# Mean squares of q and k from two float32r products of squares split in two, in a transformer-like two-layer mixer kernel

## The chip, the cores and the metric

The kernel runs on one core of a Trainium2 chip. The metric is the device time of one execution in microseconds. Several engines work at once, each through its own list of instructions: TensorE (PE) multiplies matrices, VectorE (DVE), ScalarE (ACT) and GpSimd (POOL) work elementwise, and SyncE (SP) issues most transfers. Semaphores hold an instruction back until the data that it needs are there.

## The reference

Two layers treat 1024 latent tokens and 256 prompt tokens of width 1024. A layer computes, for latent and prompt tokens alike:

```
h = rms_norm(x, norm_g) * (1 + scale) + shift        # scale, shift, gate from adaLN
aq, ak, av, ag, bq, bk, bv, bg, cx, cg, ga, gb, gc = split(h @ w_in)
qa, ka = rope(rms_norm(aq, a_qn)), rope(rms_norm(ak, a_kn))   # the prompt is not rotated
ya = attention(qa, ka, av, sink) * silu(ag)          # branch A: window of 128, 8 heads, 2 kv heads
qb, kb = rms_norm(bq, b_qn), rms_norm(bk, b_kn)
yb = attention(qb, kb, bv, bias) * silu(bg)          # branch B: 2-D neighbourhood, 8 heads
yc = lru_scan(conv(cx)) * silu(cg)                   # branch C
z = sigmoid(ga)*(ya @ w_br[0]) + sigmoid(gb)*(yb @ w_br[1]) + sigmoid(gc)*(yc @ w_br[2])
x = x + gate * (z @ w_out)
```

The change concerns the `rms_norm` of q and k: each head has 64 channels, and its vector is divided by the root of the mean of its squares plus 1e-6.

## The kernel before

Activations lie feature-major: 128 channels on the partitions, tokens along the free axis, in three chunks of 512, 512 and 256 tokens (the last is the prompt). Dense products are float32 in effect: weights and activations are each split into two float32r parts, hi and lo, and a product is three float32r products. For the weights ScalarE copies the hi part (line 415) and GpSimd subtracts for the lo part (line 416).

TensorE's order is written by a planner, the class `Weave`. It keeps a clock `now` that each emitted matrix product advances by its planned duration, holds two queues of dense jobs and a heap of steps that become due, and interleaves these with the attention of groups of heads. `W.later(T["ms"], f)` makes f due T["ms"] planned nanoseconds later. The other engines' order is made from the order in which the program emits.

q and k of a pair of heads are computed chunk by chunk in jobs; after the last product of a chunk its `evac` calls `qk_norm` (line 713). ScalarE squares the chunk (line 716), VectorE multiplies it by its gain (717). The step `finish` is due T["ms"] later: TensorE multiplies the squares by `blk`, a float32 constant that averages the 64 channels of each head (line 721). Then VectorE adds eps (723), ScalarE takes Ln and Exp (729, 730), one Newton step follows on both (731 to 734), and in branch A latent chunks are rotated: VectorE shuffles (738) and GpSimd multiplies and adds (739 to 741), with cosines and sines in a tile of tag `stage`. Last, `to_dram` splits the result in two float32r parts on GpSimd (a copy, line 751, and a subtraction, 752) in a tile `st` of tag `stage`, which goes to DRAM. `stage` has two buffers, `qraw` and `qsq` as well.

A layer has 5 jobs for k (four in branch B, one in branch A) and 8 for q. Tiles of chunk c of k and q are named `k_..._c` and `q_..._c`.

Of the kernel before, what the change touches and what calls it, by code (L numbers as in the profile page):

```python
# [9 lines left out]
F32 = mybir.dt.float32  # L10
F32R = mybir.dt.float32r
# [4 lines left out]
P = 128  # L16
# [11 lines left out]
EPS = 1e-6  # L28
# [49 lines left out]
LDB = ("d", "t")  # L78
T = dict(f1=9, f2=2, kc=3000, c0=10000, cq=1, gx=3, nx=3500, yo=1500, yi=1000, aa=2, ab=3, ap=1300, ac=3500, ms=1800, v=3000, tok=8260, scale=1000, t0=3100, tb=2000, o=2000, soft=7000, pace=9000, lg=300, lr=8000, cv=9500, le=4000)


class Weave:
    """Order of the tensor engine's work. A step is emitted once its operands should be there (times are in ns of
    the tensor engine's work); products that wait for nothing fill the time in between."""

# [34 lines left out]

    # the first job of a queue that will need weights
    def loads(self, q):
# [11 lines left out]

    # the weights of the job after this one are fetched while this one runs
    def fetch(self):
# [53 lines left out]
def trunk(nc, tc, ctx, I, K, O):  # L190
    PSUM = bass.MemoryType.PSUM
    DRAM = bass.MemoryType.DRAM
# [5 lines left out]
    cp = ctx.enter_context(pool("const"))  # L198
# [8 lines left out]

    # the loads of the start go out in the order of the program
    def ordered(ins):
# [3 lines left out]
    def f32(ap):  # L213
        return ap.bitcast(F32)

    def mm(out, a, b, start, stop):
        nc.tensor.matmul(out, a, b, start=start, stop=stop)  # L217
        n = 1
        for d in b.shape[1:]:
            n *= d  # L220
        W.now += max(n, 256) / 2.4 * (4 if a.dtype == F32 else 1) + 3
# [7 lines left out]

    # the table that serves both Exp and Ln, from the moment that x is there  # L230
    def exp_ln(x):
# [3 lines left out]

    cst = cp.tile([P, 386], F32, name="cst")
    nc.scalar.dma_start(cst[:, :384], K["k_const"][:, :384])
    nc.scalar.dma_start(cst[:, 384:], K["k_const"][:, 768:])
    ident, blk, ones_d, sel = cst[:, 0:128], cst[:, 128:256], cst[:, 256:384], cst[:, 384:386]
    fill = cp.tile([P, 2], F32, name="fill")  # L240
# [18 lines left out]

# [1 line left out]
    colT, dcol, sink, crows = [], [], [], []  # L261
# [27 lines left out]
    def constants(l):  # L289
        sk, ct, dc = sink[l], colT[l], dcol[l]  # L290
        tc.keep_in_program_order(nc.vector.tensor_scalar(sk[:, 1], sk[:, 0], -1.0, None, ALU.mult))
        # gains (those of q with the score scale) times -1 / 2, gate biases negated or halved
        for i, c in enumerate((-HD ** -0.5, 1.0, -HD ** -0.5, 1.0)):
            nc.vector.tensor_scalar(dc[:, i:i + 1], ct[:, R_QN + i:R_QN + i + 1], -0.5 * c, None, ALU.mult)
        nc.vector.tensor_scalar(dc[:, 4:12], ct[:, R_BA:R_BA + 8], -1.0, None, ALU.mult)
        nc.vector.tensor_scalar(dc[:, 12:20], ct[:, R_BX:R_BX + 8], 0.5, None, ALU.mult)
        # softplus(-lam) = max(-lam, 0) + log1p(exp(-|lam|)), log1p(y) = 2 atanh(y / (2 + y))
        lam = ct[:, R_LAM:R_LAM + 8]
        tmp = cp.tile([P, 40], F32, name=f"sp{l}", tag="sp")
        y, z, z2, acc, mx = (tmp[:, 8 * i:8 * i + 8] for i in range(5))  # L300
        nc.vector.tensor_scalar(mx, lam, -1.0, None, ALU.mult)
        nc.vector.tensor_tensor(y, lam, mx, ALU.min)
        nc.scalar.activation(y, y, AF.Exp)
        nc.vector.tensor_scalar(z, y, 2.0, None, ALU.add)
        nc.vector.reciprocal(z, z)
        nc.vector.tensor_tensor(z, z, y, ALU.mult)
        nc.vector.tensor_tensor(z2, z, z, ALU.mult)
        nc.vector.tensor_scalar(acc, z2, 1.0 / 17, 1.0 / 15, ALU.mult, ALU.add)
        for n in (13, 11, 9, 7, 5, 3, 1):
            nc.vector.tensor_tensor(acc, acc, z2, ALU.mult)  # L310
            nc.vector.tensor_scalar(acc, acc, 1.0 / n, None, ALU.add)
        nc.vector.tensor_tensor(acc, acc, z, ALU.mult)
        nc.vector.tensor_scalar(mx, mx, 0.0, None, ALU.max)
        nc.vector.scalar_tensor_tensor(acc, acc, 2.0, mx, ALU.mult, ALU.add)
        nc.vector.tensor_scalar(dc[:, 20:28], acc, -8.0, None, ALU.mult)
        nc.vector.tensor_scalar(dc[:, 28:36], acc, 8.0, None, ALU.mult)

# [1 line left out]
    mod = [cp.tile([P, 24, 2], F32, name=f"mod{l}") for l in range(DEPTH)]  # L319
# [81 lines left out]

# [1 line left out]
    def load_w(w, c0, name):  # L403
# [27 lines left out]

    # a job: one block of 128 columns of a weight matrix for the tokens of all the chunks
    # (tall: tile by tile of the contraction for all the chunks at once)
    def job(w, c0, chunks, rhs, evac, name, before=None, tall=False):
# [29 lines left out]

    # the modulated input of a layer in two parts, latent and prompt tokens in tiles of their own
    class Hidden:
# [7 lines left out]

        # room that a part of the prompt takes later
        def before(self, i, k, name):
# [19 lines left out]

    # several blocks side by side, so that each tile of H serves them all as soon as it is there
    def wide(w, blocks, ci, H, sp):
# [22 lines left out]

    # rs = (ms + EPS) ** -0.5: by Exp and Ln, then one step of Newton's
    def rstd(rs, ms, tmp):
# [6 lines left out]

# [1 line left out]
    def add_square(l, ci, k, x, acc, add):  # L532
# [29 lines left out]

# [1 line left out]
    def lru(l, H, rp):  # L564
# [4 lines left out]
        tiles = {}  # L569
# [50 lines left out]
        for f in range(4):  # L620
# [17 lines left out]
            A, S = [], []  # L638
            # r = sigmoid; a = exp(log a), log a = -8 softplus(-lam) r
            for d in range(2):  # L640
# [11 lines left out]
            for d in range(2):  # L652
                nc.scalar.activation(R[d], R[d], AF.Tanh, scale=dc[:, 28 + 4 * d + f:29 + 4 * d + f])
                # 1 - a^2 = (1 + a^2) tanh(-log a)
                nc.vector.scalar_tensor_tensor(S[d], S[d], 1.0, R[d], ALU.add, ALU.mult)
# [9 lines left out]
            for d in range(2):  # L665
                # sqrt(1 - a^2) / 2 times (1 + tanh) x = sqrt(1 - a^2) sigmoid x
                nc.scalar.activation(S[d], S[d], AF.Ln, bias=tiny_c, scale=0.25)
# [17 lines left out]

# [1 line left out]
    def gate_evac(dst, name):  # L687
# [18 lines left out]

# [1 line left out]
    def attention(l, H, ap):  # L708
        w_in = I["w_in"][l]
        loaded = []  # L710

        # normalised q and k (rotated in branch A) go to DRAM in two float32r parts
        def qk_norm(ps, N, gain, rope_c0, name, then):
# [3 lines left out]
            nc.vector.tensor_scalar(raw[:, :N], ps, gain, None, ALU.mult)  # L717

            def finish():
                ms = ps_tile("t", f"{name}_ms")  # L720
                mm(ms[:, :N], blk, sq[:, :N], True, True)
                me = cp.tile([P, 512], F32, tag="g2", name=f"{name}_me", bufs=3)
# [4 lines left out]
                rs = sq  # L727
                # one step of Newton's on rs; raw carries its factor -1 / 2
                nc.scalar.activation(rs[:, :N], me[:, :N], AF.Ln)
# [116 lines left out]
        class Keys:  # L846
            """Keys, values and biases of a pair of heads; in branch A all the pairs share keys and values."""

# [46 lines left out]
        class Group:  # L895
            """Heads a, b of a pair, query blocks t0 and t0 + 1; two parts of two units (head, block) each."""

# [24 lines left out]

            # q, masks and biases are negated, so the least score is the negated maximum
            def score(g, s, i):
# [215 lines left out]

# [1 line left out]
    def merge_jobs(l, mp, zpool, rest, swap):  # L1142
        Y, Z, acc, gated, gate = {}, [], [], {}, {}

        # y silu(g), with silu(g) = g (1 + tanh(g / 2)) / 2
        def gate_y(b, f):
# [72 lines left out]
    def output_jobs(l, cis, Z, xp, H, free):  # L1219
# [4 lines left out]
        def evac(k):  # L1224
            def run(ci, ps):
                c0, N = CHUNKS[ci]
                name = f"xo{l}_{ci}_{k}"
                # x of the prompt and its mean square lie where H is written when they are no longer needed
                if last or ci < 2:
# [26 lines left out]

    # half of the features of a chunk goes out, token-major
    def write_out(ci, xs, h):
# [12 lines left out]

# [1 line left out]
    def input_load(ci, sp):  # L1273
# [29 lines left out]

# [1 line left out]
    def bias_tables():  # L1305
# [177 lines left out]
```

## Time and profile before

| | us |
|---|---|
| median of three runs (lowest, highest) | 3311.87 (3310.23, 3314.44) |
| span of the profiled execution | 3318.7 |
| TensorE busy in it | 3198.1 |
| VectorE busy | 1767.1 |
| ScalarE busy | 1675.4 |
| GpSimd busy | 971.7 |

The profile has one execution; what it gives besides is its span, from the first to the last instruction, 0.2% longer than the median of the timed runs. A row of a timeline has a start, a duration, the engine, the line of the kernel and the tiles. Matrix products are pipelined, so that a product's duration in such a row is longer than the time for which it holds TensorE: that is read from one start to the next.

### The profile page before, as it was taken

To read this page: it belongs to the slowest core of one execution; us is meant where nothing else is said; L and a number is where in the kernel's file an instruction comes from. 1 tells how busy PE (TensorE), PEld (TensorE's weight loads), DVE (VectorE), ACT (ScalarE), POOL (GpSimd) and SP (SyncE) were. 2 spreads that over 40 slices of the span, in tenths; PEclk is the share of its full clock that TensorE was granted. 3 is DMA by queue.
4 is the path that set the end of the run, shared out by engine and by line. 5 is a ranking of instruction groups with operands and counts; after the bars stand their busy time and mean duration, and the time that the engine had idled before them with its cause. 6 is when DMAs were issued, how large, how long until landed. Compare 5 with 4: busy or idle time off the path is not lost.

```text
span 3318.7 us, 47971 instructions
## 1 busy us (share of the span) xinstructions
PE 3198.1 (96%) x17419; PEld 2657.4 (80%) x17419; DVE 1767.1 (53%) x3255; ACT 1675.4 (50%) x3565; POOL 971.7 (29%) x827
## 2 busy tenths in 40 slices
PE   8888999999999999999999999999999999999999
PEld 5655678888888888888878777888888888888887
DVE  5545236566665665445453544566656665645531
ACT  5544435555555555544245573455555555544422
POOL 3433332222232220126433233122223221112643
PEclk9989999999999999999999999999999999999999
DMA  8445463454443322365442225454445332337543
GB/s 289 118 103 117 123 185 98 140 158 119 139 144 108 99 83 85 135 215 175 129 135 91 66 69 142 128 146 138 118 143 171 99 92 82 91 103 241 184 145 102
DMA packets 414121, 435.02 MB, mean 131 GB/s; under 512 B 43872, under 2 KB 329148, under 8 KB 412604
## 3 DMA queue, kind: packets, MB, share of 16 engines
q1 hardware_dynamic: 407900, 414.91, 42.1%
q0 software_dynamic: 5664, 16.83, 1.9%
q8 instruction: 137, 2.24, 0.3%
q14 instruction: 100, 0.82, 0.1%
q10 hardware_dynamic: 320, 0.21, 0.0%
HBM read 298.12 MB, written 137.29 MB: 131 GB/s over the span
## 4 chain that ended last, share of the span: by engine, by line
PE 72%; DVE 10%; DMA 6%; ACT 4%; issue 4%; POOL 3%; SPq 1%; ACTq 0%; POOLq 0%; DVEq 0%
PE gt L217 14%; PE sg L217 10%; PE o L217 6%; PE q L217 5%; PE pt L224 5%; PE po L217 5%; PE v L217 4%; PE k L217 4%; PE br L217 4%; PE sc L217 3%; PE sl L217 3%; POOL acc L1190 2%; PE lg L217 1%; PE cx L217 1%; PE ada L348 1%
## 5 line engine op out<-in xcount | busy, mean ns | idle before, releaser
L420 ACT CAST PT<-pt 128x512 fp32r<-128x512 f32 (+2 forms) x528 | 270.1, 536 | 344.1 <-PE pt L224 341.5
L421 DVE TENSOR_TENSOR PT<-pt,PT 128x512 fp32r<-128x512 f32 (+2 forms) x528 | 319.8, 621 | 93.2 <-ACT PT L420 91.8
L944 DVE TENSOR_REDUCE st<-sc 128x1 f32<-128x512 f32 x256 | 176.3, 689 | 293.9 <-PE sc L217 293.3
L217 PE MATMUL gt<-hhl,wgt_h 128*128 128x512 f32 x736 | 303.5, 412 | 2.1 <-ACT wgt_h L415 2.1
L217 PE MATMUL gt<-hhl,wgt_l 128*128 128x512 f32 x736 | 291.9, 397 | 6.1 <-POOL wgt_l L416 6.1
L217 PE MATMUL gt<-hll,wgt_h 128*128 128x512 f32 x736 | 290.1, 394 | 0.0
L224 PE MATMUL pt<-cst,P 128*128 128x128 f32 x1856 | 271.1, 274 | 0.1
L416 POOL TENSOR_TENSOR wgt_l<-wgt_r,wgt_h 128x512 fp32r<-128x512 f32 x110 | 165.5, 1510 | 338.8 <-ACT wgt_h L415 318.4
L224 PEld LDWEIGHTS pt<-cst,P 128*128 128x128 f32 x1856 | 218.5, 141 | 3.8 <-PE pt L224 0.5
L217 PE MATMUL po<-z,wpo_h 128*128 128x512 f32 (+1 forms) x768 | 211.1, 363 | 10.0 <-ACT z L420 9.4
L217 PE MATMUL br<-yl,wbr_h 128*128 128x512 f32 (+1 forms) x576 | 205.0, 356 | 2.9 <-DVE yl L421 2.9
L217 PE MATMUL br<-yh,wbr_l 128*128 128x512 f32 (+1 forms) x576 | 204.7, 355 | 0.0
L961 ACT ACTIVATE P<-sc,st 128x512 f32<-128x512 f32 x256 | 175.4, 685 | 57.7 <-DVE st L955 57.2
L217 PE MATMUL br<-yh,wbr_h 128*128 128x512 f32 (+1 forms) x576 | 204.4, 355 | 0.0
L217 PE MATMUL sc<-Kpast,Q 128*128 128x512 f32 x512 | 170.5, 414 | 13.9 <-ACT P L961 13.9
L217 PEld LDWEIGHTS gt<-hhl,wgt_h 128*128 128x128 f32 x736 | 139.9, 190 | 47.2 <-issue 19.4
L217 PE MATMUL o<-PT,Vpast 128*128 128x256 f32 x1024 | 177.2, 295 | 0.0
L416 POOL TENSOR_TENSOR wsg_l<-wsg_r,wsg_h 128x512 fp32r<-128x512 f32 x48 | 66.5, 1394 | 368.2 <-ACT wsg_h L415 310.0
L963 ACT ACTIVATE P<-sl,st 128x384 f32<-128x384 f32 (+1 forms) x320 | 170.8, 534 | 4.9 <-DVE st L951 4.7
L217 PEld LDWEIGHTS gt<-hhl,wgt_l 128*128 128x128 f32 x736 | 139.8, 190 | 39.0 <-POOL wgt_l L416 7.0
L217 PEld LDWEIGHTS po<-z,wpo_h 128*128 128x128 f32 x768 | 137.9, 193 | 31.9 <-ACT z L420 10.3
L217 PE MATMUL sg<-hhl,wsg_h 128*128 128x512 f32 x384 | 161.7, 421 | 0.0
(340 smaller groups left out, 8611.4 us busy)
## 6 DMA issues: line engine op xcount, KB each, us to landing
Q<-q_d SPq DMA_DIRECT2D x160, 256.0 KB
gl<-g_d SPq DMA_DIRECT2D x48, 640.0 KB
wgt_r<-in_w_in_dram SPq DMA_DIRECT2D x110, 256.0 KB
g_d<-tgt SPq DMA_DIRECT2D x92, 256.0 KB
wa<-in_w_ada_dram POOLq DMA_DIRECT2D x64, 256.0 KB, 3.4
q_d<-q_st SPq DMA_DIRECT2D x64, 256.0 KB
wpo_r<-in_w_out_dram SPq DMA_DIRECT2D x64, 256.0 KB
yg<-y_d SPq DMA_DIRECT2D x24, 640.0 KB
```

Source lines behind the costliest of these rows:

```text
L217: nc.tensor.matmul(out, a, b, start=start, stop=stop)
L224: nc.tensor.transpose(out, x, idn)
L348: nc.tensor.matmul(ps[32 * j:32 * j + 32], sT[:, k], w, start=k < 4, stop=k >= 4)
L416: nc.gpsimd.tensor_sub(lo, r, f32(hi))
L420: nc.scalar.copy(hi, x)
L421: nc.vector.tensor_sub(lo, x, f32(hi))
L944: nc.vector.tensor_reduce(cm, psc, AX.X, ALU.min)
L961: nc.scalar.activation(pt[:, nl * P:(nl + 4) * P], psc, AF.Exp, bias=m, scale=-1.0, accum_out=sums[:, t, x, 1:2])
L963: nc.scalar.activation(pt[:, :nl * P], loc, AF.Exp, bias=m, scale=-1.0, accum_out=sums[:, t, x, 0:1])
L1190: nc.gpsimd.tensor_add(z, z, g)
```

## The change

The mean squares come from two float32r products. After the square, GpSimd copies it into the first half of a float32r tile `two` and subtracts this from the square for the second half; `finish` multiplies both halves by `blk_r`, the same constant in float32r, which is rounded once at the start. `two` is a third tile of tag `stage` for each chunk, beside `cs` and `st`. The delay T["ms"] goes from 1800 to 4500. The comments that the rest of the diff takes out are left away.

```
-T = dict(..., ms=1800, ...)
+T = dict(..., ms=4500, ...)
...
-    cst = cp.tile([P, 386], F32, name="cst")
-    nc.scalar.dma_start(cst[:, :384], K["k_const"][:, :384])
-    nc.scalar.dma_start(cst[:, 384:], K["k_const"][:, 768:])
-    ident, blk, ones_d, sel = cst[:, 0:128], cst[:, 128:256], cst[:, 256:384], cst[:, 384:386]
+    cst = cp.tile([P, 258], F32, name="cst")
+    nc.scalar.dma_start(cst[:, 0:128], K["k_const"][:, 0:128])
+    nc.scalar.dma_start(cst[:, 128:256], K["k_const"][:, 256:384])
+    nc.scalar.dma_start(cst[:, 256:], K["k_const"][:, 768:])
+    ident, ones_d, sel = cst[:, 0:128], cst[:, 128:256], cst[:, 256:258]
+    blk_r = cp.tile([P, P], F32R, name="blk_r")
+    blk = cp.tile([P, 512], F32, tag="g2", name="blk", bufs=3)
+    nc.gpsimd.dma_start(blk[:, :P], K["k_const"][:, P:2 * P])
+    nc.scalar.copy(blk_r, blk[:, :P])
...
             nc.scalar.activation(sq[:, :N], ps, AF.Square)
             nc.vector.tensor_scalar(raw[:, :N], ps, gain, None, ALU.mult)
 
+            two = ap.tile([P, 2, 512], F32R, tag="stage", name=f"{name}_two", bufs=2)
+            nc.gpsimd.tensor_copy(two[:, 0, :N], sq[:, :N])
+            nc.gpsimd.tensor_sub(two[:, 1, :N], sq[:, :N], f32(two[:, 0, :N]))
+
             def finish():
                 ms = ps_tile("t", f"{name}_ms")
-                mm(ms[:, :N], blk, sq[:, :N], True, True)
+                mm(ms[:, :N], blk_r, two[:, 0, :N], True, False)
+                mm(ms[:, :N], blk_r, two[:, 1, :N], False, True)
```

GpSimd's order around the first two chunks of k of branch A, before. `sq`, `raw` and `cs` are the tiles of the rotation, `st` that of the store, `wv` a weight of v.

```order
L739 TENSOR_TENSOR k_0_0_sq<-k_0_0_sq,k_0_0_cs 128x512
L740 TENSOR_TENSOR k_0_0_raw<-k_0_0_raw,k_0_0_cs 128x512
L741 TENSOR_TENSOR k_0_0_raw<-k_0_0_raw,k_0_0_sq 128x512
L751 CAST k_0_0_st<-k_0_0_raw 128x512
L752 TENSOR_TENSOR k_0_0_st<-k_0_0_raw,k_0_0_st 128x512
L416 TENSOR_TENSOR wv_0_0_l<-wv_0_r_8221,wv_0_0_h 128x512
L416 TENSOR_TENSOR wv_0_4_l<-wv_0_r_8227,wv_0_4_h 128x512
L739 TENSOR_TENSOR k_0_1_sq<-k_0_1_sq,k_0_1_cs 128x512
```

The same place after the change; `two` are the split squares.

```order
L725 CAST k_0_0_two<-k_0_0_sq 128x512
L726 TENSOR_TENSOR k_0_0_two<-k_0_0_sq,k_0_0_two 128x512
L749 TENSOR_TENSOR k_0_0_sq<-k_0_0_sq,k_0_0_cs 128x512
L750 TENSOR_TENSOR k_0_0_raw<-k_0_0_raw,k_0_0_cs 128x512
L421 TENSOR_TENSOR wv_0_0_l<-wv_0_r_8305,wv_0_0_h 128x512
L751 TENSOR_TENSOR k_0_0_raw<-k_0_0_raw,k_0_0_sq 128x512
L761 CAST k_0_0_st<-k_0_0_raw 128x512
L725 CAST k_0_1_two<-k_0_1_sq 128x512
L762 TENSOR_TENSOR k_0_0_st<-k_0_0_raw,k_0_0_st 128x512
L726 TENSOR_TENSOR k_0_1_two<-k_0_1_sq,k_0_1_two 128x512
```

The split of chunk 1's squares has come in between the two operations of chunk 0's store, and one weight split between the rotation's.

GpSimd's order at the first k of branch B of a layer, before:

```order
L416 TENSOR_TENSOR wv_0_0_l<-wv_0_r_3503,wv_0_0_h 128x512
L751 CAST k_0_0_st<-k_0_0_raw 128x512
L752 TENSOR_TENSOR k_0_0_st<-k_0_0_raw,k_0_0_st 128x512
L416 TENSOR_TENSOR wv_0_4_l<-wv_0_r_3509,wv_0_4_h 128x512
L751 CAST k_0_1_st<-k_0_1_raw 128x512
```

And after:

```order
L725 CAST k_0_0_two<-k_0_0_sq 128x512
L726 TENSOR_TENSOR k_0_0_two<-k_0_0_sq,k_0_0_two 128x512
L421 TENSOR_TENSOR wv_0_0_l<-wv_0_r_3503,wv_0_0_h 128x512
L421 TENSOR_TENSOR wv_0_4_l<-wv_0_r_3509,wv_0_4_h 128x512
L761 CAST k_0_0_st<-k_0_0_raw 128x512
L725 CAST k_0_1_two<-k_0_1_sq 128x512
L762 TENSOR_TENSOR k_0_0_st<-k_0_0_raw,k_0_0_st 128x512
L726 TENSOR_TENSOR k_0_1_two<-k_0_1_sq,k_0_1_two 128x512
L725 CAST k_0_2_two<-k_0_2_sq 128x256
```

Here too chunk 1's split stands behind the copy of chunk 0's store, and both weight splits stand ahead of it; chunk 2's split goes before chunk 1's store.

## Rows read from the trace of the kernel before

**Rows 1.** The page: the span and the busy time of each engine.
```profile
span 3318.7 us, 47971 instructions
...
PE 3198.1 (96%) x17419; PEld 2657.4 (80%) x17419; DVE 1767.1 (53%) x3255; ACT 1675.4 (50%) x3565; POOL 971.7 (29%) x827
```

**Rows 2.** Stretches: engines' busy us (instructions), granted clock, DMA; attention, a short one.
```profile
434.00:1232.00 798.00, 787.26 (x4564) 672.07 (x4562) 485.74 (x1049) 442.81 (x1127) 194.38 (x178) 0.99 0.43 126
...
1011.40:1014.80 3.40, 3.40 (x11) 2.71 (x10) 1.70 (x5) 1.06 (x3) 1.09 (x3) 0.51 0.59 142
```

**Rows 3.** Waits of TensorE and its weight loads: us, times, longest.
```profile
PE sc L217 <- ACT P L961: 13.9, 21, 1.2
...
PEld q_ms L217 <- ACT q_sq L716: 0.9, 2, 0.5
```

**Rows 4.** Single lines: count, ns min/median/max, first and last start, forms.
```profile
L723 DVE TENSOR_SCALAR q_me<-q_ms x48: 396/690/693, 458.8 to 2825.4; 128x512 f32<-128x512 f32 x32, 128x256 f32<-128x256 f32 x16
...
L723 DVE TENSOR_SCALAR k_me<-k_ms x30: 403/690/692, 441.0 to 2491.4; 128x512 f32<-128x512 f32 x20, 128x256 f32<-128x256 f32 x10
...
L716 ACT ACTIVATE q_sq<-q x48: 363/597/622, 455.5 to 2821.0; 128x512 f32<-128x512 f32 x32, 128x256 f32<-128x256 f32 x16
```

**Rows 5.** Timeline of TensorE around one mean-square product: start, us, operation.
```profile
911.88 0.63 PE L217 MATMUL sc<-Kpast,Q 128*128 128x512 f32 x2
912.34 0.52 PE L217 MATMUL sl<-Klat,Q 128*128 128x384 f32 x2
...
915.19 1.02 PE L217 MATMUL q_ms<-q_sq,cst 128*128 128x512 f32 x2
...
916.16 0.28 PE L217 MATMUL q<-hlc,wq_h 128*128 128x256 f32 x1
916.28 0.28 PE L217 MATMUL q<-hhc,wq_l 128*128 128x256 f32 x1
```

**Rows 6.** GpSimd's groups by shape: busy us, mean ns, idle before.
```profile
L752 POOL TENSOR_TENSOR q_st<-q_raw,q_st 128x512 fp32r<-128x512 f32 x32 | 42.2, 1318 | 2.6
...
L751 POOL CAST q_st<-q_raw 128x512 fp32r<-128x512 f32 x32 | 22.0, 686 | 93.7 <-DVE q_raw L734 92.8
...
L752 POOL TENSOR_TENSOR q_st<-q_raw,q_st 128x256 fp32r<-128x256 f32 x16 | 12.0, 749 | 1.3
```

**Rows 7.** Timeline of TensorE, the mean-square products of k of branch A.
```profile
878.99 1.02 PE L217 MATMUL k_ms<-k_sq,cst 128*128 128x512 f32 x2
...
889.22 1.02 PE L217 MATMUL k_ms<-k_sq,cst 128*128 128x512 f32 x2
...
895.50 0.59 PE L217 MATMUL k_ms<-k_sq,cst 128*128 128x256 f32 x2
```

**Rows 8.** Timeline of GpSimd, the copies of the stores of the same k.
```profile
890.19 0.61 POOL L751 CAST k_st<-k_raw 128x512 fp32r<-128x512 f32 x1
...
901.61 0.69 POOL L751 CAST k_st<-k_raw 128x512 fp32r<-128x512 f32 x1
```

**Rows 9.** Timeline of TensorE and GpSimd in the first pair of heads of branch B.
```profile
439.95 1.02 PE L217 MATMUL k_ms<-k_sq,cst 128*128 128x512 f32 x2
...
448.80 0.61 POOL L751 CAST k_st<-k_raw 128x512 fp32r<-128x512 f32 x1
...
457.70 1.03 PE L217 MATMUL q_ms<-q_sq,cst 128*128 128x512 f32 x2
...
463.69 0.61 POOL L751 CAST q_st<-q_raw 128x512 fp32r<-128x512 f32 x1 [5.07 <-DVE q_raw L734]
...
464.93 1.02 PE L217 MATMUL q_ms<-q_sq,cst 128*128 128x512 f32 x2
```

**Rows 10.** Timeline of VectorE, the last operation of the same normalisation as rows 7.
```profile
884.67 0.69 DVE L734 SCALAR_TENSOR_TENSOR k_raw<-k_sq,k_raw 128x512 f32<-128x512 f32 x1
```

**Rows 11.** Waits of GpSimd: us, times, longest.
```profile
POOL k_st L751 <- DVE k_raw L734: 138.7, 22, 19.1
```

**Rows 12.** Timeline of TensorE before the stretch at the lower clock.
```profile
1010.23 0.86 PE L217 MATMUL o<-PT,Vlat 128*128 128x256 f32 x5 [1.83 <-DVE PT L421]
```

More of the change, by code (lines that the diff above doesn't have):

```diff
@@ L78 @@
 LDB = ("d", "t")
-T = dict(f1=9, f2=2, kc=3000, c0=10000, cq=1, gx=3, nx=3500, yo=1500, yi=1000, aa=2, ab=3, ap=1300, ac=3500, ms=1800, v=3000, tok=8260, scale=1000, t0=3100, tb=2000, o=2000, soft=7000, pace=9000, lg=300, lr=8000, cv=9500, le=4000)
+T = dict(f1=9, f2=2, kc=3000, c0=10000, cq=1, gx=3, nx=3500, yo=1500, yi=1000, aa=2, ab=3, ap=1300, ac=3500, ms=4500, v=3000, tok=8260, scale=1000, t0=3100, tb=2000, o=2000, soft=7000, pace=9000, lg=300, lr=8000, cv=9500, le=4000)
 class Weave:
```

## The prediction

> **What bounds the kernel now.** I read the page's totals first, then the stretches, then the waits. TensorE is busy for 96% of a span of 3318.7 us, every other engine for little more than half of it or less [rows 1]. The change lies in the two attention stages, some 798 us each, since only they normalise q and k: there TensorE is busy for 787.3 of 798 us at a granted clock of 0.99, ScalarE for 443, VectorE for 486, GpSimd for 194 [rows 2]. So a product that gets shorter there shortens the kernel, and any moment that TensorE waits lengthens it. Today it hardly waits for the squares: 0.9 us in 2 waits is all that stands against them [rows 3].
>
> **What it removes.** A mean-square product is made for each chunk of q and k: 48 + 30 = 78, of them 32 + 20 = 52 of 512 columns and 26 of 256 [rows 4]. In the trace one of 512 columns starts at 915.19 and the products behind it are back in their rhythm of 0.12 us at 916.16, so it holds TensorE for 916.16 - 0.12 - 915.19 = 0.85 us [rows 5]. Two float32r products of 512 columns start at 911.88 and the next one at 912.34, which is 0.46 us for the pair [rows 5]. The change gives back 0.39 us for 512 columns, and for 256 I take half (an estimate): 52 x 0.39 + 26 x 0.19 = 25 us.
>
> **What it adds.** GpSimd gets a copy and a subtraction for each chunk. The same two operations on the same shapes stand in the trace as the split before the store: 0.69 and 1.32 us for 512 columns [rows 6]; for 256 the subtraction has 0.75 us and the copy, an estimate, 0.4. That is 52 x 2.01 + 26 x 1.15 = 134 us on an engine that is busy for 971.7 us [rows 1]: no bound by its sum. ScalarE's one copy of the constant and one more small DMA at the start lie ahead of TensorE's first transposes; I cost them at nothing, and at 2 us if that cover is gone.
>
> **Where it hurts: GpSimd's order.** The mean-square product now waits for GpSimd. By itself that would fit: square 0.6 [rows 4], copy 0.69, subtraction 1.32 [rows 6] and some 0.5 us of hand-overs (an estimate) make 3.1 us after the chunk's last product, and the new delay of 4500 planned ns is 21 products of 512 columns, which at 0.23 us each (half of the pair above) are 4.8 us of TensorE's real work. But GpSimd does its work in the order written. In the new order the store of chunk 0 (its copy) stands ahead of the split of chunk 1, and the two subtractions behind; the place shown for branch A has even the rotation, three operations, and a weight's split in front. The store of chunk 0 hangs on chunk 0's whole normalisation, which begins with chunk 0's mean-square product. So this product sets when chunk 1's squares are split, and TensorE stands before chunk 1's product until they are. This loop does not exist before.
>
> Its length can be read. With the rotation: product at 878.99, the store's copy at 890.19, so 11.2 us [rows 7, 8]. Then copy, copy, subtraction, subtraction: 2 x 0.65 + 2 x 1.3 = 3.9 us. TensorE comes to the next product after 10.24 us (878.99 to 889.22) [rows 7], and the new order leaves about as much work between them. Wait: 11.2 + 3.9 - 10.2 = 4.9 us. Three of these five places a layer also have a weight split of 1.4 us inside the loop, so I take 5.7 on average. This is each first-to-second chunk of branch A (one k and four q): 5 a layer, 10 in all, 57 us.
> Second to third chunk of branch A, where the short split stands behind the second store (3 a layer; in the other two it goes first): 12.4 us from product to copy (889.22 to 901.61), then 0.65 + 0.4 + 1.3 + 0.75 = 3.1, against 6.3 us of TensorE (889.22 to 895.50) [rows 7, 8]: 9.2 us, 6 times, 55 us.
> Without the rotation the loop is shorter. The first q of a layer: 457.70 to 463.69 is 6.0 us, 3.9 behind it, against the 7.2 us between the products (457.70 to 464.93) less the 0.4 saved: 3.1 us. The first k: 439.95 to 448.80 is 8.9 us, 3.9 behind it, against the same 6.8: 6.0 us [rows 9]. Seven such places a layer, three in the first pair of heads and one in each small chunk or q behind it, mostly nearer the second: 4 us, 14 times, 56 us.
> Sum of the waits: 57 + 55 + 56 = 168 us in 30 places; the others come out under 1.5 us or at nothing. Bounds: if a waiting TensorE leaves VectorE and ScalarE free, the loop falls towards its own work. Of the 6.4 us from product (878.99) to raw result (884.67 + 0.69) in the place shown, seven operations of nearly 0.7 us each, as the last of them, are 4.6 and the product itself 0.85 [rows 5, 7, 10], so 1 us of each loop can go, 3 in the second ones: 168 - 24 - 18 is about 125 us. If all loops are as slow as the slower of those shown (12.4 with the rotation, 8.9 without), 10 x 6.9 + 6 x 9.2 + 14 x 6.0 = 208 us.
>
> That GpSimd holds a ready operation behind one that waits shows in its idle time: 138.7 us in 22 stretches ended by the raw k of VectorE, ahead of the store's copy [rows 11]. The Trainium skill says the same in TensorE: Matmul & The Clock Gate, Architectural detail: the GpSimd queue is strict first-in first-out. By that rule the waits stand as summed; if a ready split could pass the store, they would be nothing and the sum -25 us.
> The Trainium skill's GPSIMD Engine Reference, Elementwise, gives about 2.6 cycles an element for a two-input operation, which is an estimated 1.1 us for 512 columns at its 1.2 GHz where the trace has 1.32; with two subtractions in each of 30 loops the sum would be 12 us lower by the page.
>
> **The clock.** A wait of 1.83 us before 1010.23 is followed by a stretch from 1011.4 to 1014.8 at a granted clock of 0.51, with TensorE busy throughout [rows 2, 12]: half of 3.4 us, 1.7 us lost. Nearly all of the 30 waits are longer. In 10 of them the slower work falls into the time before the next such wait and shortens it; the other 20 cost 1.7 us: 34 us (between 0 and 30 x 2.6 = 78, since a long wait may bring a second such stretch). Against that, waits for the softmax, which TensorE has now in these stages (13.9 us over the span [rows 3]), can disappear in the new ones: -10 us, between 0 and -14.
>
> **Sum.** -25 + 168 + 34 - 10 = +167 us on the profiled 3318.7: 3486. The median of the timed runs is 3311.87, 0.2% below the profiled span, so 3486 x 0.998 = 3478 us. Ends: -25 + 125 + 0 - 14 = +86 (3398) and -25 + 208 + 78 = +261 (3573).
>
> **Rivals.**
> 1. The split is ready in time (faster). One mechanism: 4.8 us of TensorE's work lie between a chunk's end and its mean-square product, and the split's own chain takes 3.1. Then only the 25 us remain, 3287 us. It decides once the store's copy is issued behind, or ends before, the next chunk's split. Against it: the order, and a loop of 11.2 us and more against 10.2. 5%.
> 2. Waits and gain cancel, within 0.2% (about what a measurement of this kernel can tell from no change): the waits would have to be 1 us a place. 3%.
> 3. The loop tightens much more than I allow, because VectorE and ScalarE, busy for 61% and 55% of these stages [rows 2], serve it at once and the clock holds: 10 x 3 + 6 x 6 + 14 x 1.5 = 87 us of waits, +62, 3374 us. For it: both engines really are freed when TensorE waits. 14%.
> 4. The waits spread: the softmax of the attention groups runs on the same VectorE and ScalarE orders, its work bunches up after each wait, and the clock falls twice. The upper ends, +261 or more, 3573 us. 12%.
> 5. The float32r products are no shorter than the float32 one, so only the 25 us don't come: 3503 us. Against it the 0.46 us for a pair of the same shape. 3%.
> My forecast of a few per cent slower has 63%.
>
> **How the numbers follow.** Faster needs rival 1: 0.05. Same is rival 2: 0.03. Slower is the rest: 0.92. The forecast's own range is 3398 to 3573. The range below reaches from rival 3's value to rival 4's, 3370 to 3580; rivals 1 and 2, and the tails of 3 and 4, lie outside it, about 2 in 10.
>
> **What would show it.** Right: TensorE's mean-square products show waits for GpSimd's subtraction of the squares, 4 to 10 us each in branch A, some 30 in all, 125 to 208 us together; GpSimd's copy of a store is what its idle time ends with just before; the granted clock of the attention stages falls from 0.99 to about 0.95; the products of the mean squares take 0.46 us a pair. The lru, merge and output stages stay as they are. Wrong: if those waits are below 1 us each, the loop is not there; if they are there and the span has not grown, something else in these stages had slack that I did not see.

## The result, and the profile after

| | before | after |
|---|---|---|
| median of four runs, us (lowest, highest) | 3313.15 (3310.23, 3317.15) | 3503.66 (3502.46, 3507.85) |
| span of the profiled execution, us | 3318.7 | 3506.1 |
| mean granted clock of TensorE | 0.984 | 0.957 |

The ratio is 1.0579, with a 95% interval from 1.0564 to 1.0594: the kernel became 5.8% slower. The profiled execution lies 187.4 us above that of before.

The page of the kernel after, with its span and the engines' busy time, answers to [rows 1]:

```profile
span 3506.1 us, 48300 instructions
...
PE 3248.1 (93%) x17419; PEld 2708.5 (77%) x17419; DVE 1750.1 (50%) x3255; ACT 1677.1 (48%) x3566; POOL 1083.9 (31%) x984
```

TensorE's busy time grew by 50 us although its products became shorter, since a part of them ran at half the clock. GpSimd has 112 us more and is still busy for less than a third.

The attention stage of the first layer, then two short stretches in it, as in [rows 2] (busy us of PE, PEld, DVE, ACT, POOL, granted clock, DMA share, GB/s):

```profile
434.00:1330.00 896.00, 813.57 (x4578) 697.16 (x4578) 481.81 (x1048) 444.84 (x1127) 259.99 (x262) 0.94 0.40 114
934.40:941.10 6.70, 4.75 (x16) 4.06 (x16) 2.09 (x4) 1.72 (x4) 3.15 (x3) 0.51 0.56 148
692.00:695.40 3.40, 3.40 (x10) 2.64 (x11) 1.88 (x4) 1.25 (x3) 0.00 (x0) 0.53 0.59 154
```

The stage is longer, TensorE is idle in it for 82 us against 11 of before, and the clock fell from 0.99 to 0.94. From a layer's first mean-square product to the first one of its last chunk it is 880 us against 790 of before, 90 us more in the first layer and 89 in the second. All else together moved by 8 us: 6.4 ahead of the first mean-square product, 0.2 between the layers, 1.7 behind the last. So the change costs what it costs in the two attention stages.

TensorE's waits (us in total, times, longest) have four new rows for the split, where [rows 3] had 0.9 us:

```profile
PE q_ms L217 <- POOL q_two L725: 59.3, 18, 5.6
PE q_ms L217 <- POOL q_two L726: 35.0, 22, 2.0
PE k_ms L217 <- POOL k_two L725: 30.4, 8, 5.8
PE k_ms L217 <- POOL k_two L726: 19.1, 12, 1.9
...
PE vt L224 <- ACT vr L819: 10.9, 2, 5.6
...
PE sc L217 <- ACT P L971: 2.6, 6, 1.1
```

The four are 143.8 us. Line 725 is GpSimd's copy of the squares, for the first of the two products, 726 the subtraction for the second. A chunk often has both waits, so 60 waits stand at 34 chunks (over 1 us each). The wait of the scores for the softmax fell from 13.9 to 2.6 us; a wait for the copy of the values, `vr`, is new, 10.9 us at two places.

One place shows the mechanism, the second chunk of k in branch A. TensorE, with the first chunk's products as the first row and the third chunk's as the last (start, us, operation, in brackets the idle time before it and what ended it):

```profile
919.36 0.71 PE L217 MATMUL k_ms<-k_two,blk_r 128*128 128x512 f32 x2 [0.19 <-DVE PT L426]
...
929.30 0.28 PE L217 MATMUL k<-hhc,wk_l 128*128 128x256 f32 x1
933.92 0.50 PE L217 MATMUL k_ms<-k_two,blk_r 128*128 128x512 f32 x1 [4.33 <-POOL k_two L725]
936.37 0.79 PE L217 MATMUL k_ms<-k_two,blk_r 128*128 128x512 f32 x1 [1.95 <-POOL k_two L726]
936.96 0.63 PE L217 MATMUL q<-hhl,wq_h 128*128 128x512 f32 x1
937.38 0.63 PE L217 MATMUL q<-hll,wq_h 128*128 128x512 f32 x1
...
950.28 0.58 PE L217 MATMUL k_ms<-k_two,blk_r 128*128 128x256 f32 x1 [5.83 <-POOL k_two L725]
```

and in the same moment VectorE, one row, and GpSimd:

```profile
926.86 0.74 DVE L748 STREAM_SHUFFLE k_sq<-k_raw 128x512 f32<-128x512 f32 x1
...
927.68 1.28 POOL L749 TENSOR_TENSOR k_sq<-k_sq,k_cs 128x512 f32<-128x512 f32 x1 [12.97 <-PE sl L217]
...
930.16 1.26 POOL L421 TENSOR_TENSOR wv_l<-wv_r,wv_h 128x512 fp32r<-128x512 f32 x1
931.38 1.26 POOL L751 TENSOR_TENSOR k_raw<-k_raw,k_sq 128x512 f32<-128x512 f32 x1
932.70 0.61 POOL L761 CAST k_st<-k_raw 128x512 fp32r<-128x512 f32 x1
933.25 0.61 POOL L725 CAST k_two<-k_sq 128x512 fp32r<-128x512 f32 x1
933.83 1.27 POOL L762 TENSOR_TENSOR k_st<-k_raw,k_st 128x512 fp32r<-128x512 f32 x1
935.05 1.26 POOL L726 TENSOR_TENSOR k_two<-k_sq,k_two 128x512 fp32r<-128x512 f32 x1
```

The first chunk's products start at 919.36. GpSimd stood idle for 13 us before that chunk's rotation, until VectorE's shuffle of the same tile ended at 927.60 (the releaser named there, a product of scores, is only the last event in time). It worked through the rotation, a weight's split and the store's copy, and only then split the squares of the second chunk, for which TensorE stood. The products behind the wait start every 0.43 us (936.96 to 937.38), as long as the clock is at 0.51.

Three quantities can be summed from a trace: the gaps between TensorE's products (idle), half of TensorE's busy time in the stretches at 0.50 of the clock (what the clock took), and the rest, which is the products' own work.

| trace | span | waits for the split | idle in all | lost to the clock |
|---|---|---|---|---|
| before | 3318.7 | none made | 108 | 43 |
| after | 3506.1 | 144 | 244 | 116 |

From TensorE's first to its last product the kernel after takes 186 us more: 136 of idle time and 73 of clock, less 23 for the shorter products.

### The profile page after: what moved, and what is told of

The parts are those of the page before. It is cut to its first block, busy times and chain, and to the rows that moved or that the text cites. A ratio compares the mean times of both kernels' runs of the same rounds, so it can differ in the third digit from the quotient of the medians.

```text
span 3506.1 us, 48300 instructions
## 1 busy us (share of the span) xinstructions
PE 3248.1 (93%) x17419; PEld 2708.5 (77%) x17419; DVE 1750.1 (50%) x3255; ACT 1677.1 (48%) x3566; POOL 1083.9 (31%) x984
## 5 line engine op out<-in xcount | busy, mean ns | idle before, releaser
L217 PEld LDWEIGHTS po<-z,wpo_h 128*128 128x128 f32 x768 | 137.5, 193 | 34.5 <-ACT z L425 10.9
```

## The experiments

Each ratio is to the kernel before, timed beside the run on the same chip (3316 to 3320 us). "Own buffers" means that the two parts of the squares no longer share the two `stage` buffers with the rotation's factors (`cs`), the stores (`st`) and the values; they take turns with the `me` tiles in three other buffers.

| run | ratio (95% interval) | waits for the split | idle in all | lost to the clock |
|---|---|---|---|---|
| e1_delay_only | 1.0068 (1.0055 to 1.0080) | none made | 126 | 48 |
| e10_pair_no_split | 1.0062 (1.0046 to 1.0078) | none made | 142 | 47 |
| e2_split_unread | 1.0169 (1.0155 to 1.0183) | not read | 147 | 56 |
| e3_split_act_dve | 1.0294 (1.0280 to 1.0308) | 85 | 186 | 76 |
| e7_split_first | 1.0162 (1.0148 to 1.0176) | 37 | 164 | 58 |
| e9_own_buffers | 1.0155 (1.0142 to 1.0169) | 24 | 155 | 65 |
| e9b_own_in_order | 1.0563 (1.0547 to 1.0579) | 156 | 254 | 104 |
| e7b_first_own | 1.0154 (1.0140 to 1.0168) | 23 | 151 | 71 |
| e8_act_own | 1.0163 (1.0149 to 1.0177) | 14 | 161 | 61 |
| e8b_act_own_3000 | 1.0077 (1.0064 to 1.0089) | 25 | 140 | 48 |
| e8d_act_own_2200 | 1.0085 (1.0071 to 1.0099) | 35 | 142 | 51 |
| e5_delay_1800 | 1.0852 (1.0835 to 1.0870) | 219 | 313 | 130 |

### The wait, or something else that came with the change

**The delay alone**, in the kernel before.

```
-T = dict(..., ms=1800, ...)
+T = dict(..., ms=4500, ...)
```

> The kernel before with the planner's delay of the mean-square product raised from 1800 to 4500 and nothing else; the float32 product stays. Theory (the price is TensorE standing before a product whose split GpSimd has not made): no such wait exists here, so 3305 to 3325 us, ratio 0.998 to 1.004, and a clock of 0.98 to 0.99. Rival (the later place of the product is itself the price, since normalised q and k reach the softmax later): a good part of the 190 us, at least 3370 us.

Measured: 3341.82 us, ratio 1.0068. The theory's range was too good by 17 us: the delay costs some 22 us by itself, without a wait for any split. It is an eighth of the change's loss, so the rival is wrong as well.

**The split made, but not read**, in the kernel before with the delay at 4500. The product, the last line here, stays as it was.

```
+            two = ap.tile([P, 2, 512], F32R, tag="stage", name=f"{name}_two", bufs=2)
+            nc.gpsimd.tensor_copy(two[:, 0, :N], sq[:, :N])
+            nc.gpsimd.tensor_sub(two[:, 1, :N], sq[:, :N], f32(two[:, 0, :N]))
...
                 mm(ms[:, :N], blk, sq[:, :N], True, True)
```

> The kernel before with the delay of 4500, and GpSimd also makes the split of the squares (copy and subtraction, in the same buffers and the same place in its order), but TensorE still multiplies the unsplit squares in one float32 product; the split is read by nobody. Theory (the wait of TensorE for the split is the price): 3310 to 3335 us, TensorE's waits for GpSimd before mean-square products under 10 us in all, although GpSimd is 134 us busier and its queue has the same order. Rival (GpSimd's load, its late stores or the two more stage buffers are the price): 3450 us or more.

Measured: 3375.04 us, ratio 1.0169, between both ranges and nearer to the theory's. GpSimd is as busy as after the change (1088.7 us), and no mean-square product waits for it. With the delay's 0.7 taken off, GpSimd's work, its order and the shared buffers cost 1.0% without anybody reading the split; the other 4% of the change appear only when TensorE reads it.

### What makes the wait

**The split on other engines**, in the kernel after: `split` is a ScalarE copy and a VectorE subtraction. The buffers stay shared.

```
-            nc.gpsimd.tensor_copy(two[:, 0, :N], sq[:, :N])
-            nc.gpsimd.tensor_sub(two[:, 1, :N], sq[:, :N], f32(two[:, 0, :N]))
+            split(two[:, 0, :N], two[:, 1, :N], sq[:, :N])
```

> The changed kernel with the squares split by a ScalarE copy and a VectorE subtraction in place of GpSimd's two. The two float32r products and the delay of 4500 stay. Theory: the split no longer stands behind a store's copy, the loop is open, the waits go (under 15 us in all) and the 25 us of shorter products remain: 3284 to 3305 us, ratio 0.992 to 0.998 to the kernel before. Rival (the pair of products is no shorter in the kernel's rhythm, or VectorE and ScalarE now make the softmax late): 3313 us or more.

Measured: 3415.68 us, ratio 1.0294: the time is in the rival's range, for another reason than the rival's, and the theory that only GpSimd's order closes the loop falls here. Half of the loss is gone, but these waits of TensorE are left:

```profile
PE q_ms L217 <- ACT q_two L425: 35.3, 16, 5.3
PE k_ms L217 <- ACT k_two L425: 29.4, 8, 9.1
PE q_ms L217 <- DVE q_two L426: 15.7, 18, 2.0
...
PE k_ms L217 <- DVE k_two L426: 5.0, 11, 0.8
```

ScalarE shows why, in the third chunk of k in branch A:

```profile
906.77 0.38 ACT L721 ACTIVATE k_sq<-k 128x256 f32<-128x256 f32 x1 [2.31 <-POOL k_raw L750]
...
919.69 0.41 ACT L425 CAST k_two<-k_sq 128x256 fp32r<-128x256 f32 x1 [6.68 <-POOL k_raw L749]
```

The squares are there at 907.2, but the copy starts at 919.69, when GpSimd's rotation has read the factors `cs` of the chunk before (line 749 there). `two` takes a `stage` buffer which that tile still holds. So there is a second loop, by way of the buffers.

**GpSimd's rotation and store written behind the next split**, in the kernel after, on the same engines. `flush`, which emits what is held, is also called behind each split and ahead of other users of the raw buffers; T["hold"] is 7000.

```
-                if rope_c0 is not None:
-                    nc.gpsimd.tensor_tensor(rs, rs, cs[:, 1], ALU.mult)
...
-                then(raw[:, :N])
+                def rest():
+                    if rope_c0 is not None:
+                        nc.gpsimd.tensor_tensor(rs, rs, cs[:, 1], ALU.mult)
...
+                    then(raw[:, :N])
+                held.append(rest)
+                W.later(T["hold"], lambda: rest in held and flush())
```

> The changed kernel with the same instructions on the same engines, but GpSimd's part of the normalisation (rotation and store) is written into its order only after the split of the next chunk's squares, or after 7000 planned ns where no chunk follows. Theory (the order of GpSimd's queue makes the loop): waits for the split fall from 144 us to under 30 us, the clock returns to 0.98 or more, 3285 to 3320 us. Rival (GpSimd is too slow for a split of 2 us in the path, wherever it stands): waits stay above 100 us, 3450 us or more.

Measured: 3372.61 us, ratio 1.0162. Waits for the split fell from 144 to 37 us, so GpSimd is not too slow for the place; the clock came back to 0.979. The theory's 3285 to 3320 were missed. This edit also changes which `stage` buffer a split gets, and it moves about a fifth of TensorE's rows in the timeline, so it does not separate order and buffers.

**Own buffers, nothing else.** The lines left away write and read `two[0]` and `two[1]` in place of the halves.

```
-            two = ap.tile([P, 2, 512], F32R, tag="stage", name=f"{name}_two", bufs=2)
+            two = [cp.tile([P, 512], F32R, tag="g2", name=f"{name}_two{i}", bufs=3) for i in range(2)]
...
```

> The changed kernel with the two parts of the squares in buffers of their own (two tiles in the rotation of the me tiles) and no longer in the pair of buffers that they share with rotation factors, stores and values; engines and GpSimd's order stay. Theory (GpSimd's order is the longer of two loops, the shared buffers the shorter): waits for the split stay at 100 us or more, 3440 to 3510 us. Rival (the shared buffers make the loop): waits under 50 us, at most 3400 us.

Measured: 3369.28 us, ratio 1.0155, with 24 us of waits: the rival's numbers. The reason stands in GpSimd's timeline, at the first and second chunk of k in branch A:

```profile
894.77 0.61 POOL L725 CAST k_two<-k_sq 128x512 fp32r<-128x512 f32 x1 [10.73 <-ACT k_sq L721]
895.46 1.85 POOL L726 TENSOR_TENSOR k_two<-k_sq,k_two 128x512 fp32r<-128x512 f32 x1
897.27 1.28 POOL L749 TENSOR_TENSOR k_sq<-k_sq,k_cs 128x512 f32<-128x512 f32 x1
...
902.36 0.61 POOL L761 CAST k_st<-k_raw 128x512 fp32r<-128x512 f32 x1
```

With a buffer free, the split of the second chunk now stands ahead of the rotation and the store of the first: the order on GpSimd did not stay the same, though the expectation had supposed that it would. No line of the order was edited, so that order follows the buffers as well as the order in which the program emits, and the shared buffers had led to the one of the changed kernel. In branch A the split takes the buffer of the `cs` of the chunk before (e3) and cannot stand ahead of the rotation that reads it; why it stood behind the store's copy too was not separated.

**Own buffers, but GpSimd's order held as written**, for the copy shown, the subtraction behind it and the store's copy.

```
-            nc.gpsimd.tensor_copy(two[0][:, :N], sq[:, :N])
+            tc.keep_in_program_order(nc.gpsimd.tensor_copy(two[0][:, :N], sq[:, :N]))
...
```

> The run with the parts of the squares in buffers of their own, which lost most of its waits, but GpSimd's split copies, split subtractions and store copies are held in the order in which the program writes them, so that a chunk's store again stands ahead of the next chunk's split, as in the changed kernel. Nothing else differs. Theory (GpSimd works strictly in order, so this order by itself makes the loop, and the shared buffers only led to it): waits for the split back at 100 us or more, 3450 to 3520 us. Rival (the shared buffers are the cause and the order harmless): waits under 40 us, 3360 to 3390 us.

Measured: 3504.62 us, ratio 1.0563, with these waits of TensorE:

```profile
PE q_ms L217 <- POOL q_two L725: 83.6, 22, 6.9
PE k_ms L217 <- POOL k_two L725: 46.7, 12, 7.2
PE q_ms L217 <- POOL q_two L726: 17.9, 22, 1.7
PE k_ms L217 <- POOL k_two L726: 7.8, 14, 1.7
```

They are 156 us, and GpSimd's rows at the same place have the store ahead of the split again:

```profile
925.81 0.61 POOL L761 CAST k_st<-k_raw 128x512 fp32r<-128x512 f32 x1
926.50 1.26 POOL L762 TENSOR_TENSOR k_st<-k_raw,k_st 128x512 fp32r<-128x512 f32 x1
927.71 0.61 POOL L725 CAST k_two<-k_sq 128x512 fp32r<-128x512 f32 x1
...
929.50 1.26 POOL L726 TENSOR_TENSOR k_two<-k_sq,k_two 128x512 fp32r<-128x512 f32 x1
```

This settles it. The same instructions with the same buffers differ by 4.0% when GpSimd's order is held, and the order with the store in front reproduces the changed kernel to 0.2%. TensorE's order is the same in both, product for product; on ScalarE 48 of 3566 instructions and on VectorE 86 of 3255 stand at another place, which nothing in the edit asked for. GpSimd's order by itself is enough for the loop. The shared buffers are a loop of their own (85 us of waits in e3, 14 with own buffers in e8), and in the changed kernel they are also what led to that order.

**Both loops open**, once on GpSimd (the edits of e7 and e9 together), once on ScalarE and VectorE (e3 and e9 together).

> GpSimd's rotation and store written behind the next chunk's split, as in the run before, and the parts of the squares also in buffers of their own: both loops open, still on GpSimd. Theory: waits for the split fall from 42 us to under 15 us; what is left over is the delay's cost (1.0068 measured) less 25 us of shorter products: 3310 to 3345 us, ratio 0.997 to 1.008. Rival (GpSimd is too slow for this place): waits stay near 40 us, 3365 us or more.

> The changed kernel with the squares split by ScalarE and VectorE and the parts in buffers of their own. Theory: the waits of 84 us that this split had with the shared buffers were for a buffer which the rotation factors of the chunk before still held; they go to under 15 us, and 3305 to 3330 us are left (the delay's 22 us less 25 us). Rival (ScalarE and VectorE are late for the softmax because of the split): 3370 us or more with the waits moved to the scores.

Measured: 3369.16 us (1.0154) and 3371.38 us (1.0163). The waits are 23 and 14 us (e7 had 37, not the 42 of the expectation), but the times are 1.5% above the kernel before, in the rivals' ranges, where the theories had nearly no loss left. Three kernels with their loops open (e9, e7b, e8) come out alike. What is left in them is in part the waits for the split; in e9 these two rows stand beside those, where before had 13.9 us and none:

```profile
PE sc L217 <- ACT P L971: 25.1, 15, 3.4
...
PE vt L224 <- ACT vr L819: 11.4, 4, 4.2
```

So of 47 us more idle time in e9, 24 are waits for the split and 23 for softmax and values; 22 us of clock come on top, and the products give back 21. In e8, whose rival expected the scores to wait, they wait for 29.8 us, but with the delay alone it is 25.1 already.

### The delay and the gain

**The changed kernel with its delay back at 1800.**

```
-T = dict(..., ms=4500, ...)
+T = dict(..., ms=1800, ...)
```

> The changed kernel with the planner's delay back at 1800, everything else as changed. Theory (at the 30 places of the loop the delay is covered by the loop, at the other 48 the split's 3.1 us is no longer covered by some 2 us of work): more places with a wait, 200 us or more of waits for the split in all, 3520 to 3640 us. Rival (the delay itself costs 22 us, as alone in the kernel before, and the loop sets all waits): 3470 to 3500 us.

Measured: 3599.24 us, ratio 1.0852, as the theory had it. The waits are 219 us, at 67 chunks, 44 of them over 1 us each. The largest row:

```profile
PE q_ms L217 <- POOL q_two L725: 109.7, 28, 9.1
```

The longer delay, which costs 22 us where nothing waits, saves some 90 us here (1.0852 against 1.0579).

**ScalarE and VectorE, own buffers, and a delay of 3000, then 2200.**

> The same with the delay at 3000 in place of 4500. Theory: the split on ScalarE and VectorE takes some 2 us and fits into the shorter delay, so the products gain 25 us and the delay costs less than its 22 us: 3290 to 3315 us, ratio 0.991 to 0.999. Rival (with less work between, TensorE waits for the split at most places, 1 us and more each, and the clock with it): 3340 us or more.

> Squares split by ScalarE and VectorE into buffers of their own, the delay at 2200. Theory (going from 4500 to 3000 gave 29 us, nearly all of it the cost of the delay, and some 10 us of that are left): 3320 to 3340 us, about the kernel before, since waits for VectorE's subtraction grow by 5 to 15 us. Rival (the waits grow by more than the delay gives back): 3350 us or more. A kernel faster than before would need waits no longer than the 25 us of 3000: 3310 us or less.

Measured: 3342.81 us (1.0077), in the rival's range, and 3346.54 us (1.0085), between both ranges. From 4500 to 3000 gives 29 us back; 2200 is no better than 3000, with overlapping intervals and waits for the split of 35 us in place of 25. Neither beats the kernel before.

**The pair of products without a split**, in the kernel after; `blk_r` is halved.

```
-            nc.scalar.activation(sq[:, :N], ps, AF.Square)
+            one = cp.tile([P, 512], F32R, tag="g2", name=f"{name}_one", bufs=3)
+            nc.scalar.activation(one[:, :N], ps, AF.Square)
...
-                mm(ms[:, :N], blk_r, two[:, 0, :N], True, False)
-                mm(ms[:, :N], blk_r, two[:, 1, :N], False, True)
+                mm(ms[:, :N], blk_r, one[:, :N], True, False)
+                mm(ms[:, :N], blk_r, one[:, :N], False, True)
```

> The changed kernel without the split: ScalarE writes the squares as float32r at once, and both float32r products read this one tile, against a constant of half the size. It leaves out the second part of the squares, the part below float32r's precision. The delay of 4500 stays, and each product waits for ScalarE's square alone, as in the kernel before. Against the run with only the delay raised (ratio 1.0068 to the kernel before, 3342 us) nothing differs but the pair of float32r products in place of one float32 product. Theory (52 x 0.39 + 26 x 0.19 us given back): 25 us less, 3310 to 3322 us, ratio 0.998 to 1.002. Rival (the pair is no shorter in the stream of products): 3335 to 3348 us.

Measured: 3339.08 us, ratio 1.0062 against 1.0068 for the delay alone: the rival's time, though not its reason. The groups of mean-square products (busy us, mean ns of one, idle before them), with only the delay raised:

```profile
L217 PE MATMUL q_ms<-q_sq,cst 128*128 128x512 f32 x64 | 32.7, 593 | 0.0
L217 PE MATMUL k_ms<-k_sq,cst 128*128 128x512 f32 x40 | 20.5, 593 | 0.0
L217 PE MATMUL q_ms<-q_sq,cst 128*128 128x256 f32 x32 | 9.8, 388 | 4.9 <-ACT q_sq L716 4.9
L217 PE MATMUL k_ms<-k_sq,cst 128*128 128x256 f32 x20 | 6.1, 388 | 1.0 <-DVE k_me L723 1.0
```

and with the pair:

```profile
L217 PE MATMUL q_ms<-q_one,blk_r 128*128 128x512 f32 x64 | 20.6, 403 | 0.0
L217 PE MATMUL k_ms<-k_one,blk_r 128*128 128x512 f32 x40 | 13.3, 414 | 0.2
L217 PE MATMUL q_ms<-q_one,blk_r 128*128 128x256 f32 x32 | 6.8, 292 | 2.8 <-DVE Y L1037 2.8
L217 PE MATMUL k_ms<-k_one,blk_r 128*128 128x256 f32 x20 | 4.4, 299 | 0.0
```

The sums are 69.1 and 45.1 us: the products are shorter by 24.0 us in all. But TensorE's idle time is 15.7 us larger (142 against 126), and the kernel is no faster. Two rows of its waits hold about 10 of them, first with the delay alone:

```profile
PE sc L217 <- ACT P L961: 25.1, 21, 3.4
...
PE vt L224 <- ACT vr L809: 3.7, 2, 1.9
```

then with the pair:

```profile
PE sc L217 <- ACT P L969: 29.8, 22, 2.5
...
PE vt L224 <- ACT vr L817: 9.1, 4, 3.1
```

TensorE waits longer for the softmax (`P`) and for the copy of the values (`vr`). Behind one of the latter stands this row of ScalarE:

```profile
940.86 0.58 ACT L817 COPY vr<-v 128x512 f32<-128x512 f32 x1 [3.76 <-POOL q_st L760]
```

`vr` shares the two `qraw` buffers with the raw q and k, which the longer delay holds until their store is split. So part of the delay's own cost is a buffer too. That row is one place. With the delay alone TensorE waits 11 us longer for the softmax than before, 5 us for `q_sq` and 4 us for `vr`, for neither of which it waited before; what makes the softmax late was not separated.

More differs between the two runs than the expectation says. The planner counts 856 ns for a float32 product of 512 columns and 433 for the pair, so it interleaves the work differently: about a fifth of TensorE's rows stand at another place. The squares have also moved to the buffers of `me`. Whether the shorter products alone, or the other order, brought the 16 us of idle time is open. But TensorE's order with the pair is that of the changed kernel, product for product. So delay, pair and this order together cost 0.6%, and the rest of the 5.8% comes with the split and its buffers.

## Why the prediction was right, and where its terms were off

The forecast was 3478 us and 5.0% slower; measured were 3503.66 and 5.8%, inside the range, on the side and by the mechanism that it named. Its steps:

- **GpSimd's order makes a loop.** Right, and shown by e9 against e9b. The step did not say why that order stood there: the third user of a pair of buffers led to it (e9), and those buffers alone make a second loop (e3). The Trainium skill (TensorE: Matmul & The Clock Gate, Architectural detail) calls GpSimd's queue strict first-in first-out for each of its cores; the 4.0% between two orders of the same instructions agree with it.
- **GpSimd's work.** 134 us more forecast; the split's own rows sum to 128, GpSimd's busy time grew by 112, and it is no bound, as said.
- **The waits.** 168 us forecast, 144 measured, within the bounds 125 to 208, at 34 chunks instead of 30. By kind, from the gaps before the mean-square products of both layers: first to second chunk of branch A 57 us, as forecast (6.3, 6.8, 4.0, 5.7 and 5.8 us in a layer, mean 5.7); second to third chunk 37 us against 55 (7.2, 4.3 and 6.9 where 9.2 stood); without the rotation 50 us against 56, over more places and from 1 to 5 us each. The second term failed for a reason that it had not priced: it took TensorE's work between the two products from the full clock, 6.3 us. At 950.28 in the trace after, TensorE worked for 7.5 us from the end of the pair at 936.96 to the start of the idle time at 944.45, since part of it ran at half the clock; the loop itself, 15.8 us from the product at 936.37 to the end of the split, was as forecast (15.5). The forecast sign named the subtraction; 90 of the 144 us stood against the copy, which itself stands behind the store.
- **The clock.** 34 us forecast, 73 measured, close to the upper bound of 78. This is the term most off. The step took one stretch of 3.4 us after each of 20 waits, from the row after a wait of 1.83 us [rows 2, 12]. The waits here came in pairs, one before each product, and the stretches behind them were mostly longer: 12 of the 16 in the first attention stage last 6.8 or 10.2 us (one of the 16 stands at the wait of 5.6 us for `vr`). In both stages 32 stretches last 205 us together, against 4 with 14 us before.
- **The gain.** The products gave 24 us of the 25 forecast (e10 against e1). That this shortens the kernel by as much did not show: with the delay at 4500 the kernel with the shorter products is only 0.06% faster, within both intervals. The step read the busy share of 787 of 798 us [rows 2] as room for the gain; with the shorter products the waits for softmax and values grew by 10 us, though whether by them or by the other order of TensorE's work is open.
- **The delay.** It was treated as cover for the split and costed at nothing beyond that. Alone it costs 0.68%; in the changed kernel it is worth some 90 us.
- **Softmax waits** fell by 11.3 us, with -10 forecast. The new wait of 10.9 us for `vr`, which no term had, took as much back.
- **The constants at the start**, costed at nothing or 2 us: TensorE's first product starts 1.3 us later (8.8 against 7.5).

From first to last product the measured sum is 136 + 73 - 23 = 186 us against the forecast 167. The idle part was forecast 22 us too high (168 - 10 against 136), the clock 39 too low, and the errors partly cancelled: that the sum came so close is luck in part.

Of the rivals, the first (the split is ready in time) needed the split ahead of the store; e9 has that order and is still 1.6% slower than before, so the rival's 3287 us were out of reach for other reasons than the one argued: 24 us of waits that stay, later softmax and values, and the clock. The second needed waits of 1 us a place; they are 4.2 on average. The third (the loop tightens) has no support in the place shown: the loop was 15.8 us against 15.5, and the wait got shorter because TensorE's own work got longer. The fourth had the clock right, that it falls for longer than one stretch, and the waits wrong. The fifth is refuted by the 24 us; that its 3503 us are the measured time is coincidence.

No kernel that was tried beats the one before.

## What to carry to other kernels

Before a step is put on an engine that is idle on average, look at what stands ahead of it in that engine's order and whether that depends on the step's own earlier result: such a loop costs, at each turn, what other work does not cover of its length, here 144 us of waits for an engine that is busy for 31% of the span. A third user of a pair of rotating buffers can bring this about without a line of the order being edited. And do not count a shorter instruction on the busiest engine as time saved: here 24 us of products came back as 16 us of idle time, though with another order of the work, on an engine that was 99% busy.

## What was not expected of the hardware

- Idle time of TensorE of 1.5 us (before 691.83, a second product's wait for the subtraction) was already followed by a stretch of 3.4 us at half the clock (the row at 692.00: 0.53, TensorE busy throughout). Before 577.60, at the same place of another job, 1.5 us of idle time had no such stretch behind it: the products there start every 0.26 us, not 0.43. Pairs of waits with 4 to 7 us together brought stretches of 6.8 and 10.2 us, some of which began inside the wait.
- The cost of the clock grows with the waits: 73 us of clock on 136 us of idle time in the changed kernel, 87 on 205 with the delay of 1800, 22 on 47 in e9 (each against the kernel before). In these about half of the idle time comes on top of it; where no product waits for a split it is less, 4 us on 34 in e10.
- Having a 0.6 us copy and a 1.3 us subtraction of the next chunk ahead of a store, in the same engine's order, was worth 135 us (e9b to e9), though the engine is busy for 31 and 33% of the span.
